# Up projections of a SwiGLU FFN token-major as seven products, with the weight sums made in DRAM by a chain of accumulating transfers

## The chip, the cores and the metric

The kernel runs on one core of a Trainium2 chip. The core has a matrix engine (TensorE, PE; its weight loads are shown apart as PEld), VectorE (DVE), ScalarE (ACT), GpSimd (POOL) and SyncE (SP), each with its own queue of instructions that it works through in order. Data moves between DRAM and the on-chip buffer (SBUF) by DMA transfers, which SP, ACT and POOL issue; TensorE writes its results into PSUM, of which the kernel uses eight tiles of 128 x 512 f32. The metric is the time of one execution in device microseconds.

## What is computed

Two layers of a decoder trunk on 512 tokens of width 1024. Each layer mixes tokens in four branches (the "mixer": a gated convolution, sparse attention, a gated recurrence, attention into a memory), adds the result to the residual `x`, and then runs a SwiGLU FFN of width 2816. The change is in the FFN:

```python
DEPTH = 2; SEQ = 512; D_MODEL = 1024; FFN_DIM = 2816
...
for l in range(DEPTH):
    x = hybrid_layer(x, ...)          # ends with:
...
    x = x + merged @ w_out
    hf = rmsnorm(x, norm_ffn)
    gate, up = jnp.split(hf @ ffn_w_up, 2, axis=-1)
    return x + (jax.nn.silu(gate) * up) @ ffn_w_down
```

All of it is f32.

## The kernel before

**Matrix products.** Every f32 operand is split in two: `hi`, a rounded copy that ScalarE makes, and `lo = x - f(hi)`, which VectorE makes. A product is three matmuls, hi x hi, hi x lo and lo x hi (`mm3`). Weights come from DRAM by loads on SP's queue into `w_raw` (two buffers, a third called `w_raw7` inside the FFN), are split into `w_hi` and `w_lo` (three buffers of 1024 columns each), and go to TensorE. `Chunk` does this for ordinary weights, `split` for the blocks of `down`.

**Order.** The code gives a program order and priorities; a scheduler fixes the order of each engine's queue when the kernel is built. Nothing is reordered at run time, so an instruction that waits holds all that stand behind it on its engine or queue.

**The FFN's up part.** `h` (the normalised input without its factor 1/rms, feature-major: 128 features on the partitions, 512 tokens along the row) is multiplied by chunks of 256 columns of the gate weights and of the up weights (`features`): 11 chunks `fc` of each, 2 x 8 x 3 matmuls of 512 columns per weight chunk. VectorE multiplies each result by `r_b`, the factor 1/rms broadcast over the partitions, ScalarE applies silu to the gates, VectorE multiplies by the up half, and the product, feature-major, is the left operand of the down projection.

**The FFN's down part.** `down` computes a 2 x 2 block product (token halves A11, A12, A21, A22; column halves C1, C2 of the weights) with seven products instead of eight (the Winograd form of Strassen's scheme). It needs sums of blocks on both sides: `operands` makes the left sums, and `weight_sums` the four right ones for each pair of 128-row blocks. Before the change, `weight_sums` loads the four blocks of one pair by a transfer on GpSimd's queue, VectorE makes four subtractions of 128 x 512, and a second GpSimd transfer stores the four sums in DRAM (`wt_dram`), from where `down` loads them. Layer 0 works in parts of 5 and 4 pairs with seven products and 2 pairs plainly (`add_down`, which also makes the next layer's input); layer 1 in parts of 6 and 5 pairs. Each `down` adds its PSUM banks into `acc` (tokens x 1024 columns) by `evict`, on VectorE. `acc` is zeroed by GpSimd in layer 0; in layer 1 it starts from `x`, brought in by `x_in` and turned by transposes on TensorE.

**What else the steps touch.** `conv_branch` (the mixer's gated convolution) multiplies the output of its first weight chunk by `r_b` into two `gate` tiles, near the start of each layer's mixer. GpSimd's queue carries, beside the weight sums, the loads of `x` in the FFN (`x_chunk`, `x_in`), a few zeroings of buffers in the mixer, the memset of `acc`, and two stores of the output. `norm_feature` makes `r_b` by matmuls against ones, `norm_token` the same factor with tokens on the partitions.

## Time and profile before

| | us |
|---|---|
| runs shown: median (lowest to highest of 3) | 2029.88 (2029.35 to 2030.08) |
| the profiled execution, its own time | 2032.38 |
| its span in the trace | 2030.6 |
| data moved by DMA | 269.86 MB, mean 133 GB/s |
| layer 0: mixer until 696.6, FFN from there | 696.6 |
| layer 1: FFN from about | 1676.6 |

The page gives, for each engine, the time in which it was busy and its share of the span. The chain of waits is followed back from the last instruction: at each step to what released it. The groups give, for one line, engine and shape: how often, the busy time in us, the mean duration of one in ns, and how long the engine had been idle before and for whom. Issues of transfers give the number, the size of each and the median time from issue to landing. Records of matmuls are pipelined and overlap; their spacing is read from the starts.

### The profile page before, as it was taken

How to read it: one execution, taken by the hardware profiler on the slowest of the kernel's cores; microseconds unless marked ns; L12 is line 12 of the kernel's file. 1: busy time of each engine (PE TensorE's matmuls, PEld its weight loads, DVE VectorE, ACT ScalarE, POOL GpSimd, SP SyncE). 2: the span in 40 equal slices, each digit the busy share in tenths (PEclk: the TensorE clock that was granted, in tenths of full speed). 3: DMA queues.
4: the chain of work that ended last, by engine and by line, in shares of the span. 5: the costliest groups of instructions: out<-in, count | busy, mean ns of one | idle time of the engine just before them, and what ended most of it. 6: DMA issues, size and time to landing. Idle time of an engine off the chain costs nothing.

```text
span 2030.6 us, 26664 instructions
## 1 busy us (share of the span) xinstructions
PE 2013.9 (99%) x10100; PEld 1690.6 (83%) x10100; DVE 1427.9 (70%) x2774; ACT 1067.2 (53%) x1914; POOL 45.1 (2%) x86
## 2 busy tenths in 40 slices
PE   8999999999999999999999999999999999999999
PEld 8998987778888888888889898877888788888887
DVE  5768898648776576666556889955678566666666
ACT  7653664866666433334345455477667544333333
POOL 0000000000000000000000000000000000000000
PEclk9999999999999999999999999999999999999999
DMA  7633231222233554664352223232222445566644
GB/s 253 210 92 104 68 104 62 83 63 83 83 113 124 196 210 150 229 218 143 105 182 72 91 79 94 73 94 68 79 80 80 151 140 192 187 212 220 222 148 155
DMA packets 192159, 269.86 MB, mean 133 GB/s; under 512 B 5774, under 2 KB 157920, under 8 KB 189088
## 3 DMA queue, kind: packets, MB, share of 16 engines
q1 hardware_dynamic: 176320, 208.51, 32.2%
q0 software_dynamic: 9568, 46.80, 6.2%
q10 hardware_dynamic: 6144, 12.87, 1.7%
q8 instruction: 79, 1.29, 0.3%
q14 instruction: 48, 0.39, 0.1%
HBM read 232.50 MB, written 35.65 MB: 132 GB/s over the span
## 4 chain that ended last, share of the span: by engine, by line
PE 95%; DVE 2%; ACT 1%; DMA 1%; issue 0%; DVEq 0%; SPq 0%; ACTq 0%
PE mm L277 28%; PE mm L279 28%; PE mm L278 27%; PE at L279 1%; PE at L278 1%; PE at L277 1%; PE tr L737 1%; PE tr L731 1%; PE at L705 1%; PE at L706 1%; ACT w_hi L97 1%; PE tr L279 1%; PE tr L277 1%; PE tr L278 1%; DVE acc L1264 0%; DVE w_lo L230 0%
## 5 line engine op out<-in xcount | busy, mean ns | idle before, releaser
L277 PE MATMUL mm<-h_hi,w_hi 128*128 128x512 f32 x1664 | 651.7, 393 | 3.1 <-ACT w_hi L97 2.4
L278 PE MATMUL mm<-h_lo,w_hi 128*128 128x512 f32 x1664 | 652.6, 392 | 0.0
L279 PE MATMUL mm<-h_hi,w_lo 128*128 128x512 f32 x1664 | 648.5, 392 | 1.7 <-DVE w_lo L230 1.6
L97 ACT ACTIVATE w_hi<-w_raw 128x1024 fp32r<-128x1024 f32 (+1 forms) x384 | 394.7, 1033 | 383.8 <-PE mm L278 242.7
L230 DVE TENSOR_TENSOR w_lo<-w_raw,w_hi 128x1024 fp32r<-128x1024 f32 x304 | 369.6, 1219 | 198.5 <-ACT w_hi L97 198.0
L277 PEld LDWEIGHTS mm<-h_hi,w_hi 128*128 128x128 f32 x1664 | 313.0, 188 | 69.4 <-ACT w_hi L97 3.9
L279 PEld LDWEIGHTS mm<-h_hi,w_lo 128*128 128x128 f32 x1664 | 313.1, 188 | 66.8 <-DVE w_lo L230 3.2
L278 PEld LDWEIGHTS mm<-h_lo,w_hi 128*128 128x128 f32 x1664 | 313.0, 188 | 63.2 <-issue 0.2
L1088 DVE TENSOR_TENSOR w_lo<-w_raw,w_hi 128x1024 fp32r<-128x1024 f32 (+1 forms) x80 | 86.5, 1090 | 64.1 <-ACT w_hi L97 64.1
L279 PE MATMUL mm<-w_hi,h_lo 128*128 128x256 f32 (+2 forms) x368 | 109.3, 297 | 0.0
L278 PE MATMUL mm<-w_lo,h_hi 128*128 128x256 f32 (+2 forms) x368 | 109.1, 297 | 0.0
L277 PE MATMUL mm<-w_hi,h_hi 128*128 128x256 f32 (+2 forms) x368 | 108.7, 298 | 0.0
L97 ACT ACTIVATE a_hi<-fg 128x512 fp32r<-128x512 f32 (+1 forms) x84 | 48.5, 580 | 112.7 <-DVE fg L1238 84.8
L277 PE MATMUL mm<-y_hi,w_hi 128*128 128x512 f32 x256 | 100.5, 394 | 1.2 <-ACT y_hi L97 1.2
L279 PE MATMUL mm<-y_hi,w_lo 128*128 128x512 f32 x256 | 100.4, 393 | 0.0
L278 PE MATMUL mm<-y_lo,w_hi 128*128 128x512 f32 x256 | 100.3, 392 | 0.0
L97 ACT ACTIVATE prob<-prob,small 128x128 f32<-128x128 f32 (+3 forms) x128 | 68.9, 554 | 17.5 <-DVE small L720 12.6
L278 PEld LDWEIGHTS mm<-w_lo,h_hi 128*128 128x128 f32 x368 | 70.1, 191 | 2.1
L279 PEld LDWEIGHTS mm<-w_hi,h_lo 128*128 128x128 f32 x368 | 70.1, 191 | 1.9
L277 PEld LDWEIGHTS mm<-w_hi,h_hi 128*128 128x128 f32 x368 | 69.8, 191 | 1.9
L97 ACT ACTIVATE gate_e<-gate 128x512 f32<-128x512 f32 x64 | 40.2, 628 | 43.5 <-DVE gate L537 42.8
L278 PE MATMUL mm<-w_lo,a_hi 128*128 128x512 f32 x160 | 62.2, 389 | 0.0
(404 smaller groups left out, 3298.6 us busy)
## 6 DMA issues: line engine op xcount, KB each, us to landing
w_raw<-in_w_in_dram SPq DMA_DIRECT2D x72, 1024.0 KB, 5.2
w_raw<-in_ffn_w_up_dram SPq DMA_DIRECT2D x44, 1024.0 KB, 5.2
w_raw<-in_ffn_w_down_dram POOLq DMA_DIRECT2D x20, 1024.0 KB, 5.9
w_sums<-w_raw POOLq DMA_DIRECT2D x20, 1024.0 KB, 4.5
w_raw<-in_w_lift_dram SPq DMA_DIRECT2D x32, 512.0 KB, 3.4
w_raw<-w_sums SPq DMA_DIRECT2D x20, 768.0 KB, 4.2
w_raw<-in_ffn_w_down_dram SPq DMA_DIRECT2D x9, 1024.0 KB, 6.0
w_raw<-in_mem_w_kv_dram SPq DMA_DIRECT2D x8, 1024.0 KB, 5.2
```

What stands on the lines that cost most here:

```text
L97: i = act.activation(dst, src, func, **kw)
L230: dve.tensor_sub(lo, raw[:, k:e], f(hi))
L277: return [pe.matmul(ps, ah, bh, start=first, stop=False, skip_group_check=more), pe.matmul(ps, ah, bl, start=False, stop=False, skip_group ...
L278: pe.matmul(ps, ah, bl, start=False, stop=False, skip_group_check=more),
L279: pe.matmul(ps, al, bh, start=False, stop=last, skip_group_check=more)]
L705: return [pe.matmul(ps, q[:, hh, s], k[0][:, :n], start=True, stop=False), pe.matmul(ps, q[:, hh, s], k[1][:, :n], start=False, stop=True)]
L706: pe.matmul(ps, q[:, hh, s], k[1][:, :n], start=False, stop=True)]
L731: pe.transpose(pp[:, (2 * e + i) * P:(2 * e + i + 1) * P], probs[2 * i + e][:, b * P:(b + 1) * P], ident)
L737: pe.matmul(pv[e * HD:(e + 1) * HD, :], vt[:, b, :], pt[:, b, e * 2 * P:(e + 1) * 2 * P], start=b == 0, stop=b == t)
L1088: follow(dve.tensor_sub(lo[:, k:k + n, :], src, f(hi[:, k:k + n, :])), earlier)
```

## The change

- `up_set` replaces the chunks of the up part. One set covers 512 gate columns and the 512 up columns that belong to them. Its left blocks are halves of the tokens and of the 1024 features, its right blocks the upper and lower half of the features for gate and for up. It makes seven products (A11, A12, S2, S1, S3, S4, A22) of 24 matmuls each, with the tokens on the partitions of the result ("token-major"). There are five sets; the last 256 features go through `up_plain`, 256 columns wide.
- `left_sums` makes the left sums S1 to S4 of `h` once per layer on VectorE and ScalarE.
- The results being token-major, the factor 1/rms becomes a scalar per partition (`r_t`, `nr_t`); `norm_feature` is no longer called here, `norm_token` is. `turned` brings the products back to feature-major by transposes on TensorE and a copy on ScalarE.
- `weight_sums` is called once per layer, from the convolution branch, for all sums of the layer: the up sums into a new DRAM tensor `up_sums` and the down sums into `w_sums`. Each sum is a plain copy DRAM to DRAM and an accumulating transfer on top of it, both on GpSimd's queue, and each transfer waits for the landing of the one before. The signs are arranged so that only additions are needed; `operands`, `left_sums` and `evict` carry the other signs.
- `down` works on pairs (0, 1, 10), (2, 3, 4, 5) and (6, 7, 8, 9), in layer 0 with 8 and 9 plain.
- The zeroings that stood on GpSimd in the mixer move to VectorE; the loads of `x` in the FFN move from GpSimd's queue to SP's. The memset of `acc` stays on GpSimd.

```diff
                 for u, ps in zip(us, features(w, h, (0, 1))):
-                    pool.memset(u[:, 0:2], 0.0)
+                    dve.memset(u[:, 0:2], 0.0)
                     with tc.high_priority(offset=AHEAD):
-                        dve.tensor_mul(u[:, 2:], ps, r_b)
+                        i = dve.tensor_mul(u[:, 2:], ps, r_b)
+                if c2 == 0:
+                    weight_sums(l, i)
...
-    def weight_sums(fp, l, i):
-        raw = fp.tile([P, 4, 512], F32, name="w_raw7")
-        nc.gpsimd.dma_start(raw.rearrange("p (e c) n -> p e (c n)", e=2),
-                            ffn_w_down[l][2 * i * P:2 * (i + 1) * P, :].rearrange("(e p) n -> p e n", p=P))
-        b12, b11, b22, b21 = (raw[:, j, :] for j in range(4))
-        dve.tensor_sub(b11, b12, b11)
-        dve.tensor_sub(b12, b22, b12)
-        dve.tensor_sub(b22, b22, b11)
-        dve.tensor_sub(b21, b21, b22)
-        nc.gpsimd.dma_start(wt_dram[l, :, i], raw)
+    def weight_sums(l, gate):
+        last = [gate]
+        def move(dst, src, **kw):
+            i = nc.gpsimd.dma_start(dst, src, **kw)
+            tc.add_manual_dep(i.ins, last[0].ins.name, sync, reason="one by one")
+            last[0] = i
+        def four(sums, b11, b21, b12, b22):
+            t3, t1, t2, t4 = sums
+            for dst, one, two in ((t1, b11, b12), (t2, t1, b22), (t4, t2, b21), (t3, b12, b22)):
+                for add in (False, True):
+                    for d, x, y in zip(dst, one, two):
+                        if add:
+                            move(d, y, accum_op=OP.add)
+                        else:
+                            move(d, x)
+        for n in range(FF // 512):
+            def block(e, g):
+                c = g * FF + n * 512
+                b = ffn_w_up[l][e * 512:(e + 1) * 512, c:c + 512].rearrange("(k p) n -> p k n", p=P)
+                return [b[:, 0:2, :], b[:, 2:4, :]]
+            four([[wu_dram[l, n, j][:, 0:2, :], wu_dram[l, n, j][:, 2:4, :]] for j in range(4)],
+                 *(block(e, g) for g in range(2) for e in range(2)))
+        rows = ffn_w_down[l].rearrange("(i e p) n -> p i e n", e=2, p=P)
+        for i in ((0, 2), (10, 11), (2, 4), (4, 6), (6, 8)) + (((8, 10),) if l == DEPTH - 1 else ()):
+            i = slice(*i)
+            four([[wt_dram[l, :, i, j]] for j in range(4)],
+                 *([rows[:, i, e, c]] for c in (C1, C2) for e in range(2)))
...
+    def left_sums(fp, h):
+        raw = fp.tile([P, NT, D], F32, name="acc").rearrange("p a b -> p (a b)").rearrange("p (k s) -> p k s", s=S)
+        for k in range(0, KD, 2):
+            dve.tensor_add(raw[:, k:k + 2, :], f(h[0][:, k:k + 2, :]), f(h[1][:, k:k + 2, :]))
+        g0, g1 = raw[:, 0:4, :], raw[:, 4:8, :]
+        s2, s1 = g0[:, :, :HALF], g0[:, :, HALF:]
+        dve.tensor_sub(s1, g1[:, :, HALF:], s1)
+        dve.scalar_tensor_tensor(s2, s1, -1.0, s2, op0=OP.mult, op1=OP.subtract)
...
+            def product(bank, o, src, first):
+                raw = raw_tile(fp).rearrange("p (k n) -> p k n", n=512)
+                nc.sync.dma_start(raw, src)
+                for e in range(2):
+                    w = split([(0, 2, raw[:, 2 * e:2 * e + 2, :])])
+                    for t, ps in enumerate(bank):
+                        for j in range(2):
+                            k = 2 * e + j
+                            a = [where[o](x, k)[:, t * P:(t + 1) * P] for x in lefts]
+                            mm3(ps, a, w[j], first and k == 0, k == 3, not first)
...
+                product(ba, A11, block(0, 0), True)
+                g = copies(ba, "fg", 2)
+                product(bb, A12, block(1, 0), True)
...
+                        dve.tensor_add(g[t], g[t], bb[t])
+                        A(g[t], g[t], AF.Silu, scale=r_t[:, t:t + 1])
...
+                product(ba, S2, sums[SUM2], False)
+                v = copies(ba, "fu", 4)
+                product(bc, S1, sums[SUM1], True)
+                u = copies(bc, "fu", 4)
+                product(ba, S3, sums[SUM3], False)
...
+                product(bc, S4, block(1, 1), False)
...
+                        dve.tensor_add(v[t], v[t], bc[t])
+                        dve.scalar_tensor_tensor(v[t], v[t], nr_t[:, t:t + 1], g[t], op0=OP.mult, op1=OP.mult)
+                product(ba, A22, sums[SUM4], False)
...
+            def turned(us, j, name="fx", bufs=2):
+                ps = tr_ps()
+                for t in range(NT):
+                    pe.transpose(ps[:, t * P:(t + 1) * P], us[t][:, j * P:(j + 1) * P], ident)
+                g = fp.tile([P, S], F32, name=name, bufs=bufs)
+                A(g, ps, AF.Copy)
+                return g
...
+            for part, idx in enumerate(((0, 1, 10), (2, 3, 4, 5), (6, 7, 8, 9))):
+                if part == 0:
+                    us = up_set(0, lambda: kept.append(turned(up_plain(0, [at_ps(), at_ps()]), 0, "fy", 1)))
...
+                    acc = fp.tile([P, NT, D], F32, name="acc")
+                    if last:
+                        x_in(0)
+                        x_in(4)
+                    else:
+                        pool.memset(acc, 0.0)
+                    ops.append(operands(fp, kept[0], turned(pls, 0), False, N_OPS))
+                else:
+                    ops = pairs_of(up_set(2 * part - 1), False)
+                    ops += pairs_of(up_set(2 * part), part == 2 and not last)
```

More of the change, by code (lines that the diff above doesn't have):

```diff
@@ L1128, in operands, with down @@
         return hi, lo
-    def down(fp, w2d, sums, ops, evict):
+    def down(fp, w2d, sums, idx, ops, evict):
         n = len(ops)
@@ L1184, in down @@
             raw = raw_of(2 * m)
-            nc.sync.dma_start(raw[:, 0::2, :], sums[:, i0:i0 + m, SUM3])
-            nc.sync.dma_start(raw[:, 1::2, :], rows[:, i0:i0 + m, 1, C2])
+            nc.sync.dma_start(raw[:, 0::2, :], sums[:, idx[i0]:idx[i0] + m, SUM3])
+            nc.sync.dma_start(raw[:, 1::2, :], rows[:, idx[i0]:idx[i0] + m, 1, C2])
             for i in range(m):
@@ new lines, in ffn @@
+            hs, h1 = left_sums(fp, h)
+            where = {A11: lambda x, k: x[0][:, k, :HALF], A12: lambda x, k: x[0][:, 4 + k, :HALF],
+                     A22: lambda x, k: x[0][:, 4 + k, HALF:], S2: lambda x, k: x[1][:, k, :],
+                     S1: lambda x, k: x[2][:, k, :], S4: lambda x, k: x[1][:, 4 + k, :],
+                     S3: lambda x, k: x[1][:, 8 + k, :]}
+            lefts = [(h[e], hs[e], h1[e]) for e in range(2)]
+            def product(bank, o, src, first):
+                raw = raw_tile(fp).rearrange("p (k n) -> p k n", n=512)
+                nc.sync.dma_start(raw, src)
+                for e in range(2):
+                    w = split([(0, 2, raw[:, 2 * e:2 * e + 2, :])])
[4 more added lines that the diff above has]
+                            mm3(ps, a, w[j], first and k == 0, k == 3, not first)
@@ new lines, in turned, with pairs_of @@
+            def turned(us, j, name="fx", bufs=2):
+                ps = tr_ps()
+                for t in range(NT):
+                    pe.transpose(ps[:, t * P:(t + 1) * P], us[t][:, j * P:(j + 1) * P], ident)
+                g = fp.tile([P, S], F32, name=name, bufs=bufs)
+                A(g, ps, AF.Copy)
+                return g
+            def pairs_of(us, plain):
+                return [operands(fp, *(turned(us, 2 * i + j) for j in range(2)), plain, N_OPS) for i in range(2)]
+            acc = None
@@ L1268, in evict @@
                     return adds
-                down(fp, wd, wt_dram[l, :, f0:f1], ops, evict)
-        return None, None
+                n = 2 if part == 2 and not last else len(idx)
+                down(fp, ffn_w_down[l], wt_dram[l], idx[:n], ops[:n], evict)
+            if last:
+                return None, None
+            h2, ssq2 = new_h(), new_ssq()
+            add_down(x_chunk, ffn_w_down[l][idx[n] * 256:(idx[-1] + 1) * 256, :], [Pairs(t) for t in zip(*ops[n:])],
+                     2 * len(ops[n:]), acc, h2, ssq2, lambda c: g_mix(l + 1, c))
+            return h2, ssq2
     for l in range(DEPTH):
```

149 lines of the change are left out of this document (96 added, 53 removed).

## The prediction

> **What bounds the kernel now.** I read the page's busy times and its chain of waits first, then the busy time of each engine by stretches, then single rows.
>
> ```profile
> PE 2013.9 (99%) x10100; PEld 1690.6 (83%) x10100; DVE 1427.9 (70%) x2774; ACT 1067.2 (53%) x1914; POOL 45.1 (2%) x86
> ...
> PE 95%; DVE 2%; ACT 1%; DMA 1%; issue 0%; DVEq 0%; SPq 0%; ACTq 0%
> ```
>
> TensorE is the bound: busy for 99% of the span and 95% of the chain that ended last. The stretches say that this holds in the FFN too: layer 0's up projections (697 to 806), the part of `down` behind them (806 to 860), and the tail with layer 1's end. Columns: length, busy time and instructions of PE, weight loads, VectorE, ScalarE and GpSimd, the granted clock, the DMA engines' share and rate.
>
> ```profile
> 697.00:806.00 109.00, 108.82 (x480) 89.74 (x480) 73.30 (x103) 40.81 (x54) 5.61 (x9) 1.00 0.56 195
> 806.00:860.00 54.00, 53.65 (x237) 43.97 (x236) 39.26 (x50) 21.50 (x24) 1.97 (x3) 1.00 0.60 200
> ...
> 1820.00:2030.00 210.00, 206.12 (x908) 169.88 (x906) 136.00 (x180) 73.84 (x89) 7.41 (x12) 1.00 0.55 188
> ```
>
> TensorE waits 0.5 us in the first two together. A seven-product stage (the second row) already runs at 99% of PE with VectorE at 39.26 / 54 = 73%. So a matmul that goes is worth its spacing, if nothing new makes TensorE wait. Matmul records last 0.39 us but overlap; the spacing is read from starts.
>
> ```profile
> 1729.74 0.39 PE L279 MATMUL mm<-h_hi,w_lo 128*128 128x512 f32 x1
> ...
> 1741.98 0.39 PE L279 MATMUL mm<-h_hi,w_lo 128*128 128x512 f32 x1
> ...
> 63.34 0.28 PE L278 MATMUL mm<-w_lo,mt_hi 128*128 128x256 f32 x1
> ...
> 66.33 0.28 PE L279 MATMUL mm<-w_hi,mt_lo 128*128 128x256 f32 x1
> ...
> 1721.49 1.31 PE tr L1220 x12
> ...
> L1220 PE MATMUL tr<-ident,w_raw 128*128 128x128 f32 x32 | 4.1, 272 | 0.0
> ```
>
> Between the first two starts lie 54 steps: 12.24 / 54 = 0.2267 us for 512 columns. Between the next two lie 25 steps: 2.99 / 25 = 0.120 us for 256 columns. Twelve transposes take 1.31 us of the chain: 0.109 us each, though one's own record lasts 272 ns.
>
> **The change, part by part.** *Matmuls.* Before, one layer's up projections are 11 chunks x 2 weights x 2 x 8 x 3 = 1056 matmuls of 512 columns. After, they are 5 sets x 7 products x 24 = 840, and 192 of 256 columns for the last 256 features. Over two layers: 432 fewer of 512 (-97.9 us) and 384 more of 256 (+46.1). The results are now token-major, so each set is turned by 16 transposes and the rest by 8: 88 a layer, 176 x 0.109 = +19.2. If a transpose cost the 0.272 us of its own record it would be +47.9; the twelve above stand among matmuls as the new ones will, so I take 0.109. The `norm_feature` matmuls that go and the `norm_token` ones that come are a dozen: nothing. `down` multiplies as many pairs by seven products as before (9 and 11). Sum: **-32.6 us**.
>
> *VectorE and ScalarE.*
>
> ```profile
> L230 DVE TENSOR_TENSOR w_lo<-w_raw,w_hi 128x1024 fp32r<-128x1024 f32 x187 | 228.1, 1222 | 139.4 <-ACT w_hi L97 139.2
> ...
> L1235 DVE TENSOR_TENSOR fg<-mm,rstd 128x512 f32<-128x512 f32 x44 | 29.8, 688 | 24.7 <-PE mm L279 24.5
> ...
> L1102 DVE TENSOR_TENSOR w_raw<-w_raw 128x512 f32<-128x512 f32 x20 | 13.7, 686 | 0.2
> L97 ACT ACTIVATE w_hi<-w_raw 128x1024 fp32r<-128x1024 f32 x247 | 260.6, 1058 | 292.6 <-PE mm L278 186.7 <-PE mm L279 32.6 <-PE at L279 27.4
> ```
>
> Seven blocks instead of four for the same weights: 148 splits of 1024 for 88. A set has 14 splits (14 x 1.222 = 17.1 us of VectorE), 10 operations of 512 (6.9) and two `operands` (about 4 each, from the same 0.69): 32 us beside 168 x 0.2267 + 1.7 = 39.8 of TensorE, 80%. ScalarE has 14 x 1.058 and about 20 operations of 0.63: 27 us. The 80 subtractions of the weight sums (55 us) go. So these edits cost nothing under TensorE's time, but with less cover than the 73% above. `left_sums`, 12 VectorE operations of 1024 (14.7 us) and four ScalarE copies, lies under A11, A12 and the first plain product, (48 x 0.2267 + 96 x 0.120) = 22.4 us; the first product that needs it comes behind them. Where the cover fails is at seams: end of a set, plain part to `down`, and one `down` more in each layer (three where layer 1 had two). Lower bound 0; upper bound twice the idle share of the worst stretch above (3.9 of 210), over two FFNs of some 354 us (1676.6 to 2030.6 in layer 1): 26. I take **+8** (about 2 us at each of four seams, near the rows' 0.35 in 54).
>
> *The chain of sums.* GpSimd now issues 120 transfers in layer 0 and 128 in layer 1, each waiting for the one before: 16 for each of five up blocks, 8 for each down group, half plain copies, half additions into DRAM, 512 KB but for eight of 256. The first waits for the convolution's second product:
>
> ```profile
> 109.69 0.67 DVE L594 TENSOR_TENSOR gate<-mm,rstd 128x512 f32<-128x512 f32 x1
> ...
> 1121.01 0.69 DVE L594 TENSOR_TENSOR gate<-mm,rstd 128x512 f32<-128x512 f32 x1
> ...
> L277 PE MATMUL mm<-mg_hi,w_hi x64: 389/389/389, 653.1 to 695.9; 128*128 128x512 f32 x64
> L277 PE MATMUL mm<-h_hi,w_hi x160: 389/389/497, 696.6 to 805.7; 128*128 128x512 f32 x160
> ...
> L277 PE MATMUL mm<-mg_hi,w_hi x64: 389/389/389, 1633.3 to 1676.1; 128*128 128x512 f32 x64
> ```
>
> So the chain starts at 110.4 and 1121.7, and the FFNs at 696.6 and about 1676.6. In the built kernel's order layer 0's memset of `acc` stands on GpSimd *behind all 120 links*; the first eviction of `down` adds into `acc`, and behind those adds VectorE holds every weight split, so TensorE stops soon after. That eviction is due at 696.6 + 38.1 (a set) + 23.0 (two plain products) + 2.6 (24 transposes) + 8.2 (36 matmuls) = 768.5. Allowed: (768.5 - 110.4) / 120 = **5.48 us a link**. In layer 1 there is no memset; SP's load of the first down sums waits for link 96, due about 1676.6 + 38.1 + 23.0 + 2.6, so (1740.3 - 1121.7) / 96 = 6.44. The first up sums (link 16) are never near. What a link costs is not in the trace; the nearest rows:
>
> ```profile
> w_raw<-in_ffn_w_down_dram POOLq DMA_DIRECT2D x20, 1024.0 KB, 5.9
> w_sums<-w_raw POOLq DMA_DIRECT2D x20, 1024.0 KB, 4.5
> ...
> w_raw<-in_ffn_w_down_dram SPq DMA_DIRECT2D x9, 1024.0 KB, 6.0
> ...
> w_raw<-in_ffn_w_down_dram SPq DMA_DIRECT2D x15, 512.0 KB, 3.3
> ...
> 725.97 0.56 POOL L1103 DMA_DIRECT2D w_sums<-w_raw  x1 [13.06 <-DVE w_raw L1102]
> 731.01 0.71 POOL L1096 DMA_DIRECT2D w_raw<-in_ffn_w_down_dram  x1 [4.49 <-DMA w_sums<-w_raw]
> ...
> POOL w_raw L1096 <- DMA w_sums<-w_raw: 60.8, 14, 5.3
> ```
>
> The last rows are a link already: GpSimd issues a 1 MB store and the next transfer waits for it, 0.56 + 60.8 / 14 = 4.9 us with the DMA engines at 56 to 65%. A 512 KB copy lies between the load's 3.3 and that 4.9: I take 4.2. An addition reads two blocks and writes one: at least the copy's 4.2, at most a 1 MB load and a 1 MB store link one after the other, 10.8; I take the 1 MB load, 5.9, since the block written is small beside what is read. Mean 5.05 (3.8 to 7.9): layer 0's chain ends at 110.4 + 606 = 716, 52 us early. Cost **0**; without that cover, 120 x (link - 5.48).
>
> The Trainium skill's "DMA: Bandwidth & Descriptors", "Anatomy of one DMA — SWDGE (gpsimd) path", gives about 2.0 us and the bytes at 436 GB/s for a transfer of this queue. Its "Collectives: The Full Stack", "The bandwidth ceiling: the fold count and why AG ≠ RS ≠ AR", says an adding transfer reads two sources and so moves at half the rate. By both (an estimate) a link is 3.2 or 4.4, mean 3.8, and the sum is the same; the 4.9 measured for 1 MB is a little over the first rule's 4.4.
>
> *What the chain does to the loads.* Through the mixers it adds traffic where the DMA engines are about a quarter busy (0.28 in the first row).
>
> ```profile
> 110.00:250.00 140.00, 140.00 (x882) 126.45 (x881) 113.16 (x306) 71.44 (x170) 0.20 (x2) 1.00 0.28 87
> ...
> w_raw<-in_w_in_dram SPq DMA_DIRECT2D x72, 1024.0 KB, 5.2
> ...
> w_raw<-in_w_lift_dram SPq DMA_DIRECT2D x32, 512.0 KB, 3.4
> ...
> w_raw<-in_w_out_dram SPq DMA_DIRECT2D x8, 1024.0 KB, 5.0
> ...
> SPq L219 <- DVE w_lo L230: 1277.7, 132, 19.9
> ...
> ACT w_hi L97 <- DMA w_raw<-in_w_in_dram: 8.7, 5, 3.5
> ```
>
> Loads are issued when a buffer comes free, about 9.7 us after the one before, and a split waited for one only five times. I take **+4** (0 to 15: each of the 112 loads of those three rows late by 0.14). The sums' loads are 7 MB a set, 1 MB per 5.4 us, three buffers deep. The FFN's x chunks move from GpSimd's queue to SP's, since GpSimd's is now held by waits; the zeroings move to VectorE: some 24 short operations, nothing.
>
> The profiled execution took 2032.4 us, 2.5 over the median. 2032.4 - 32.6 + 8 + 0 + 4 = 2011.8; against the median, **2009**.
>
> **The rivals.** *A, the chain is late (slower).* Everything above 5.48 us a link is paid 120 times, in front of the memset. For it: the additions are unmeasured, and links run beside the mixers' loads; against it: the 4.9 us for twice the bytes. With additions at 8.2 (a 1 MB load, and half a store of 4.5) and copies at 4.2, a link is 6.2: 120 x 0.72 = 86, 2095. It turns gain into loss from (2029.9 - 2009) / 120 = 0.17 over, at 5.65.
>
> A rule that would lengthen links is in the skill's "SBUF — State Buffer", "Who interferes with whom": VectorE's two-port copies block GpSimd, which writes the descriptors. Here GpSimd's issues last 0.56 and 0.71 us in the rows above with VectorE 70% busy, which speaks against it; one blocked copy of 1.2 a link would give 6.25 and 2009 + 92 = 2101, a case inside A with 0.02 of its chance.
>
> *B, contention.* The chain slows the mixers' loads until splits wait. 0.4 us at 112 loads is 45, in place of 4: 2050. For it: lift chunks of 5.4 us of TensorE follow 3.4 us loads; against it: the five waits above.
>
> *C, seams.* VectorE at 80% is late by 0.2 us at each of 140 half products: 28 us in place of 8, 2029, no change. Against it: the 73% stage lost 0.35 us in 54.
>
> *D, transposes at 0.272*: 2009 + 29 = 2038. The twelve above speak against it.
>
> **How the numbers follow.** Forecast 0.59, A 0.25, B 0.07, C 0.07, D 0.02. 2009 is the likeliest; its own range is 1997 (seams 0, loads 0: 2032.4 - 32.6 - 2.5) to 2024 (seams 18, loads 9). The whole range goes up to 2068, a link of 5.97 in A, leaving most of the rest of A out. What a measurement can tell from no change is about 0.2%, 4 us. Faster: the forecast and small parts of B and C, 0.64; same: most of C, the turn of A, 0.06; slower: 0.30.
>
> **What would show it.** Right: TensorE about 33 us less busy, GpSimd's transfers 4 to 6 us apart, the memset of `acc` ahead of about 760, no wait of VectorE's `acc` adds on GpSimd, up sets of about 40 us. Wrong: transfers over 5.5 us apart with TensorE idle in front of layer 0's first eviction (A); idle at splits behind loads in the mixers (B); idle spread over the sets (C); transposes in rows of 0.27 (D).

## The result, and the profile after

| | before | after |
|---|---|---|
| median of 4 runs, us | 2029.62 (2029.22 to 2030.08) | 2115.89 (2107.61 to 2121.16) |
| profiled execution: time, span, us | 2032.4, 2030.6 | 2107.6, 2105.5 |

The change made the kernel slower: 1.0421 times the time (95% interval 1.0384 to 1.0459), 86 us more where 21 fewer were forecast. One of the four executions of the run with the memset alone, further down, was slow (2485.56 us at a clock of 0.75), so its figures are the median of the other three, 2048.92, where the later expectations name 2049.8, and its stretches are read from other runs. The page of after shows the same two parts as before: busy times, and the engines' shares of the chain that ended last.

```profile
PE 1999.7 (95%) x10240; PEld 1680.3 (80%) x10240; DVE 1476.5 (70%) x2814; ACT 1190.6 (57%) x2100; POOL 230.2 (11%) x264
...
PE 59%; DMA 33%; issue 3%; DVE 3%; ACT 2%; POOL 0%; SPq 0%; DVEq 0%; POOLq 0%; ACTq 0%
```

TensorE's instructions went up by 140, as the count of the prediction has it (432 fewer of 512 columns, 384 more of 256, 176 transposes and a dozen of the norms). But TensorE is busy for 95% of the span, and a third of the chain is DMA. The waits say where (engine, line, what for; total, times, longest):

```profile
POOL up_sums L1107 <- DMA up_sums<-in_ffn_w_up_dram: 641.4, 115, 8.2
...
PE mm L283 <- DVE acc L1407: 63.7, 2, 62.9
DVE acc L1407 <- POOL acc L1392: 63.6, 1, 63.6
```

One wait of 63.6 us: VectorE's first addition into `acc` waits for GpSimd's memset, and TensorE's matmul for VectorE. GpSimd's own timeline, and after it the stretches around the stall (length, busy PE, weight loads, VectorE, ScalarE, GpSimd, granted clock, DMA share and rate):

```profile
831.53 0.72 POOL L1107 DMA_DIRECT2D w_sums<-in_ffn_w_down_dram  x1 [5.42 <-DMA w_sums<-in_ffn_w_down_dram]
836.19 1.13 POOL L1107 DMA_DIRECT2D w_sums<-in_ffn_w_down_dram  x1 [3.94 <-DMA w_sums<-in_ffn_w_down_dram]
836.89 3.95 POOL L1392 MEMSET acc<- 128x4096 f32 x1
```

```profile
697.00:770.00 73.00, 70.53 (x409) 62.45 (x408) 50.95 (x61) 41.15 (x57) 10.80 (x12) 0.98 0.82 231
770.00:840.00 70.00, 8.42 (x38) 6.29 (x36) 7.19 (x14) 7.71 (x15) 14.89 (x14) 0.60 0.53 108
840.00:900.00 60.00, 56.16 (x237) 45.57 (x238) 40.84 (x50) 26.49 (x31) 0.84 (x1) 0.96 0.57 189
```

The chain starts at 113.4 and issues its last link at 836.2: 723 us for 119 spacings, 6.07 each. The memset stands behind them, so `acc` is ready at 840.9 where VectorE wanted it at 777.3. That is rival A. What one link takes is read from the starts: a copy is issued in 0.72 us, an addition in 1.14 to 1.16.

```profile
518.17 0.72 POOL L1107 DMA_DIRECT2D up_sums<-in_ffn_w_up_dram  x1 [6.51 <-issue]
522.43 1.16 POOL L1107 DMA_DIRECT2D up_sums<-in_ffn_w_up_dram  x1 [3.54 <-DMA up_sums<-in_ffn_w_up_dram]
529.22 1.14 POOL L1107 DMA_DIRECT2D up_sums<-in_ffn_w_up_dram  x1 [5.62 <-DMA up_sums<-in_ffn_w_up_dram]
535.76 0.57 POOL L1107 DMA_DIRECT2D up_sums<-up_sums  x1 [5.41 <-DMA up_sums<-in_ffn_w_up_dram]
```

A copy of 4.26, then additions of 6.79 and 6.54: this is a quick piece of the chain. Over the whole of layer 0's chain a copy takes 5.0 us on average and an addition 7.2, from start to start (eight of the 120 links are of 256 KB). There is a second loss, in layer 1, where no memset waits: the stretch 1800 to 1840, SP's queue in it, and two pieces of the chain.

```profile
1800.00:1840.00 40.00, 26.88 (x134) 22.66 (x134) 20.68 (x35) 21.40 (x37) 6.70 (x7) 0.87 0.72 189
```

```profile
SPq L1272 <- PE tr L1276: 9.9, 1, 9.9
```

```profile
1815.99 5.60 DMA w_raw<-x_spill
...
1825.26 5.35 DMA w_raw<-in_ffn_w_down_dram
```

TensorE idles 13 of these 40 us. `x_in`'s two loads of 1 MB now stand on SP's queue, in a buffer that the weights use too; the second waits until the first has been transposed, and `down`'s first weights wait behind it.

### The profile page after: what moved, and what is told of

Same layout as the page of the kernel before. It is cut to its first block, busy times and chain, and to the rows that moved or that the text cites. A ratio compares the mean times of both kernels' runs of the same rounds, so it can differ in the third digit from the quotient of the medians.

```text
span 2105.5 us, 27445 instructions
## 1 busy us (share of the span) xinstructions
PE 1999.7 (95%) x10240; PEld 1680.3 (80%) x10240; DVE 1476.5 (70%) x2814; ACT 1190.6 (57%) x2100; POOL 230.2 (11%) x264
## 4 chain that ended last, share of the span: by engine, by line
PE 59%; DMA 33%; issue 3%; DVE 3%; ACT 2%; POOL 0%; SPq 0%; DVEq 0%; POOLq 0%; ACTq 0%
DMA up_sums<-in_ffn_w_up_dram 18%; PE mm L283 15%; PE mm L284 15%; PE mm L285 15%; DMA w_sums<-in_ffn_w_down_dram 8%; DMA up_sums<-up_sums 4%; PE at L285 2%; PE at L284 2%; PE at L283 2%; DMA w_sums<-w_sums 2%; DVE acc L1407 1%; ACT w_hi L99 1%; PE tr L283 1%; DVE w_lo L1097 1%; PE tr L284 1%
## 5 line engine op out<-in xcount | busy, mean ns | idle before, releaser
L99 ACT ACTIVATE w_hi<-w_raw 128x1024 fp32r<-128x1024 f32 (+2 forms) x444 | 456.5, 1035 | 368.9 <-PE mm L284 117.1
L283 PE MATMUL mm<-h_hi,w_hi 128*128 128x512 f32 x960 | 378.1, 395 | 2.8 <-ACT w_hi L99 1.7
L284 PE MATMUL mm<-h_lo,w_hi 128*128 128x512 f32 x960 | 378.4, 394 | 0.0
L285 PE MATMUL mm<-h_hi,w_lo 128*128 128x512 f32 x960 | 376.4, 393 | 1.3 <-DVE w_lo L236 1.3
L1097 DVE TENSOR_TENSOR w_lo<-w_raw,w_hi 128x1024 fp32r<-128x1024 f32 (+1 forms) x220 | 256.1, 1175 | 155.8 <-ACT w_hi L99 155.8
L236 DVE TENSOR_TENSOR w_lo<-w_raw,w_hi 128x1024 fp32r<-128x1024 f32 (+1 forms) x224 | 272.0, 1217 | 113.1 <-ACT w_hi L99 111.9
L1107 POOL DMA_DIRECT2D up_sums<-in_ffn_w_up_dram x120 | 121.4, 1012 | 1086.0 <-DMA up_sums<-in_ffn_w_up_dram 516.4
L283 PEld LDWEIGHTS mm<-h_hi,w_hi 128*128 128x128 f32 x960 | 180.8, 188 | 40.4 <-ACT w_hi L99 2.2
L285 PEld LDWEIGHTS mm<-h_hi,w_lo 128*128 128x128 f32 x960 | 180.9, 189 | 37.9 <-DVE w_lo L236 1.7
L284 PEld LDWEIGHTS mm<-h_lo,w_hi 128*128 128x128 f32 x960 | 180.8, 188 | 35.6 <-issue 0.2
L284 PE MATMUL mm<-w_lo,h_hi 128*128 128x256 f32 (+2 forms) x600 | 197.4, 329 | 2.1 <-DVE w_lo L1097 2.1
L283 PEld LDWEIGHTS mm<-w_hi,h_hi 128*128 128x128 f32 x600 | 113.7, 191 | 10.2 <-ACT w_hi L99 0.9
```

What stands on the lines that cost most here:

```text
L99: i = act.activation(dst, src, func, **kw)
L236: dve.tensor_sub(lo, raw[:, k:e], f(hi))
L283: return [pe.matmul(ps, ah, bh, start=first, stop=False, skip_group_check=more), pe.matmul(ps, ah, bl, start=False, stop=False, skip_group ...
L284: pe.matmul(ps, ah, bl, start=False, stop=False, skip_group_check=more),
L285: pe.matmul(ps, al, bh, start=False, stop=last, skip_group_check=more)]
L1097: follow(dve.tensor_sub(lo[:, k:k + n, :], src, f(hi[:, k:k + n, :])), earlier)
```

## The experiments

Times are medians, each set against the runs of the kernel before on the same chip (2028.8 to 2029.8); "over before" is that difference. After is 86.3 over before.

### The memset alone

```diff
-                        pool.memset(acc, 0.0)
+                        dve.memset(acc, 0.0)
```

> One edit: layer 0's memset of acc goes from GpSimd to VectorE, so nothing of down's first eviction is queued behind the 120 links any more; the links themselves stay as they are. Theory (the late memset alone makes the stall; the links are slow but otherwise in time): the wait of 63.6 us of VectorE's acc addition on GpSimd is gone, no other wait takes its place (SP's first down sums need only link 96, which came at about 700), the granted clock stays at 1.00 there, and the time falls from 2107.6 by 63.6 and some 5 to 10 us of slow clock: about 2037 (2030 to 2048). The links' spacing stays near 6.05 us. Rival (links of 6 us are too late for other users as well): SP's loads of w_sums wait instead, and the time stays above 2080. Rival (what is slow is the FFN's new order itself): the wait moves to other places of the FFN and the time stays above 2060.

Measured: 2048.92, 20.2 over before (ratio 1.0096, 1.008 to 1.0113). One word moved takes 66 us out, so the late memset is the stall. But 2048.9 lies above the 2030 to 2048 expected: 20 us over before remain where the prediction, with its chain in time, had 21 under it.

### Larger links, the memset left where it was

```diff
-                return [b[:, 0:2, :], b[:, 2:4, :]]
-            four([[wu_dram[l, n, j][:, 0:2, :], wu_dram[l, n, j][:, 2:4, :]] for j in range(4)],
+                return [b]
+            four([[wu_dram[l, n, j]] for j in range(4)],
```

> The memset of acc stays on GpSimd behind the whole chain; only the size of the up links changes: 1 MB instead of twice 512 KB, so layer 0's chain has 80 links for 120 with the same bytes. From the links measured by themselves (1 MB: copy 5.6, addition 9.3 alone, 6.8 and 9.9 beside loads; 512 KB: 5.3 and 7.9 beside loads; 256 KB some 4.7) the chain takes 20 x 6.2 + 20 x 9.6 + 32 x 6.3 + 8 x 4.7 = 555 us, from 113 to about 668, some 100 us ahead of the first eviction of down. Theory (the stall is the chain's length past the memset's due time, nothing else): the acc addition waits for nothing on GpSimd and the time is that of the run with the memset on VectorE, about 2047 (2038 to 2056). Rival (bytes set the chain's length, not links): the chain ends near 830 as before and the time stays at 2110. Rival (1 MB links hold the loads up more): no stall at acc, but over 2060.

Measured: 2046.81, 17.2 over before (1.0081, 1.0064 to 1.0099). GpSimd's timeline has the last link at 674.7 (668 was worked out), and now the memset waits for VectorE's `left_sums`, not VectorE for the memset:

```profile
674.66 1.15 POOL L1107 DMA_DIRECT2D w_sums<-in_ffn_w_down_dram  x1 [6.12 <-DMA w_sums<-in_ffn_w_down_dram]
727.20 3.53 POOL L1392 MEMSET acc<- 128x4096 f32 x1 [51.40 <-DVE hs_lo L1247]
```

The same bytes in 80 links instead of 120 end 160 us earlier, and the stall goes. The chain's length past one due time sets the loss; with a third fewer links and the bytes unchanged, that length falls from 723 to 558 us.

### Links by themselves

The kernel holds nothing but two runs of links, the second beside paced loads.

```diff
...
+    for r in range(6):
+        for k in (slice(0, 2), slice(2, 4)):
+            move(sums[0][:, k, :], block(0, r * 512)[:, k, :])
+        for k in (slice(0, 2), slice(2, 4)):
+            move(sums[0][:, k, :], block(1, r * 512)[:, k, :], accum_op=OP.add)
+    for r in range(6):
+        move(sums[1], block(0, r * 512))
+        move(sums[1], block(1, r * 512), accum_op=OP.add)
...
```

> None of the reference is computed but a copy of x: the kernel only issues links from GpSimd's queue, each behind the one before, twice: first alone, then beside loads of 1 MB of w_in on SP's queue, one every 9 to 10 us as in the mixers. In each half: 12 copies and 12 additions of 512 KB from rows of 2 KB, 6 of each with 1 MB, 6 of each with 256 KB. Theory (an addition into DRAM is slow by itself): alone, a copy of 512 KB takes 4 to 4.5 us from start to start and an addition 6 to 7, and beside the loads each is at most 0.5 us longer. Rival (the links are slow because the mixers' loads take the DMA engines): alone 4 and 5, as the sum of the prediction had it or less, beside the loads 5 and 7. The three sizes give the fixed part: if 256 KB takes more than two thirds of what 512 KB takes, a link is mostly fixed time, and 1 MB links would cost less per byte.

GpSimd's timeline in the first half, with no other transfer running: additions, copies and the next addition of 512 KB; then a 1 MB copy, an addition, and the next copy.

```profile
68.20 1.14 POOL L85 DMA_DIRECT2D sums<-in_ffn_w_up_dram  x1 [5.67 <-DMA sums<-in_ffn_w_up_dram]
74.94 0.72 POOL L85 DMA_DIRECT2D sums<-in_ffn_w_up_dram  x1 [5.60 <-DMA sums<-in_ffn_w_up_dram]
79.17 0.71 POOL L85 DMA_DIRECT2D sums<-in_ffn_w_up_dram  x1 [3.52 <-DMA sums<-in_ffn_w_up_dram]
83.63 1.16 POOL L85 DMA_DIRECT2D sums<-in_ffn_w_up_dram  x1 [3.74 <-DMA sums<-in_ffn_w_up_dram]
...
187.03 0.75 POOL L85 DMA_DIRECT2D sums<-in_ffn_w_up_dram  x1 [8.41 <-DMA sums<-in_ffn_w_up_dram]
192.62 1.14 POOL L85 DMA_DIRECT2D sums<-in_ffn_w_up_dram  x1 [4.84 <-DMA sums<-in_ffn_w_up_dram]
201.98 0.77 POOL L85 DMA_DIRECT2D sums<-in_ffn_w_up_dram  x1 [8.23 <-DMA sums<-in_ffn_w_up_dram]
```

Means of start to start, in us (the 512 KB copies alone hold two of 8.1 and 7.2 at the very start; their median is 4.27):

| | copy 256 KB, 512 KB, 1 MB | addition 256 KB, 512 KB, 1 MB |
|---|---|---|
| alone | 3.3, 4.8, 5.6 | 4.6, 6.9, 9.3 |
| beside loads | 4.9, 5.3, 6.8 | 4.6, 7.9, 9.9 |

An addition of 512 KB takes 6.9 us with nothing beside it, so it is slow by itself. Beside the loads it takes 0.9 more, and a copy 1.0 more than its median alone, so the theory's 0.5 was short and its rival has a part too. From 512 KB to 1 MB an addition grows by 2.4 us, and from 256 KB to 512 KB, half the step in bytes, by 2.3: one fixed part doesn't fit all three sizes. An addition of 256 KB takes two thirds of one of 512 KB, so the runs don't show that an addition is mostly fixed time; but the larger link is the cheaper one per byte at every step. VectorE does nothing in this kernel and GpSimd's issues last 0.72 and 1.14 us as in after: VectorE's work isn't what lengthens them.

### No chain at all

```diff
-                if c2 == 0:
-                    weight_sums(l, i)
...
-                product(ba, S2, sums[SUM2], False)
+                product(ba, S2, block(0, 1), False)
```

> The transfers that make the sums of weights are left out altogether (all 248), and the products that used sums read plain blocks of the same weights in the same sizes, so the output differs from the reference's; the matmuls, splits, transposes and loads stay. Theory (only the late memset and x's loads cost something, the chain's traffic costs the mixers nothing): the acc addition waits for nothing, mixers take 582 to 587 us and 623 us as in both kernels, and the time is that of the run with the memset on VectorE within 6 us: about 2035 (2025 to 2045). Rival (the chain's traffic slows the loads by contention): over 15 us below that run. Rival (the seven-product order itself is what costs): above 2060.

The loads keep their bytes, though one of `down`'s is made in two pieces. Measured: 2037.21, 8.4 over before (1.0037, 1.0024 to 1.005) and 11.7 under the memset alone. The time is inside 2025 to 2045, but the theory had put this run within 6 us of the other. So the chain's traffic costs something, and the seven-product FFN is slow with no sums to wait for. The traces (table under "The sum") put 4.7 of the 11.7 into the FFNs and nothing into layer 1's mixer; layer 0's mixer takes 700.6 us without a chain and 699.3 to 705.5 with it. TensorE in the stretches at the start of the first `down` of either layer:

```profile
755.00:780.00 25.00, 20.70 (x127) 18.20 (x126) 14.52 (x28) 14.56 (x26) 0.00 (x0) 0.93 0.20 69
...
1738.00:1770.00 32.00, 22.24 (x110) 18.33 (x109) 17.64 (x32) 20.21 (x36) 0.00 (x0) 0.84 0.30 98
```

4.3 us idle in layer 0, 9.8 in layer 1, at a lowered clock besides. Pieces of the chain at the two places (start, length, what):

```profile
766.44 1.22 DVE w_lo L1095
...
768.00 0.94 DVE a_lo L1145 x2
...
769.27 0.52 DVE fu L1359 x2
...
770.99 0.27 DVE fu L1359
771.31 0.50 PE mm L283
...
1752.81 4.85 DMA w_raw<-x_spill
...
1760.50 3.64 DMA w_raw<-in_ffn_w_down_dram
```

In layer 0, `down`'s first matmul waits for a bank that the second plain part's gate (`fu`) still reads; that gate stands on VectorE behind the operands of the set. In layer 1 the `x` loads come on top. The next runs take these one at a time.

### The second plain part inside the set

```diff
-                    us = up_set(0, lambda: kept.append(turned(up_plain(0, [at_ps(), at_ps()]), 0, "fy", 1)))
-                    b0 = mm_ps()
-                    pls = up_plain(1, [b0, tr_ps()])
...
+                    def plain1():
+                        pls = up_plain(1, [mm_ps(), tr_ps()])
+                        pair.append(operands(fp, kept[0], turned(pls, 0), False, N_OPS))
+
+                    us = up_set(0, plain0, plain1)
...
```

> Memset on VectorE; and the second plain part of the first set (96 matmuls of 256 columns, its gate and its operands) stands behind the set's third product instead of at the set's end, so that VectorE's and ScalarE's work for it lies under four more products. Theory (TensorE's 6 us of lost time between 755 and 780 in layer 0, and as much in layer 1, are the plain part's gate and operands waiting behind a backlog of VectorE with no product left to hide them): the stretch loses under 3 us in each layer and the time is 5 to 9 us under the run with the memset alone (2049.8), about 2043. Rival (the loss is the start of down itself, its first split and the turned operands of the set): within 3 us of 2049.8.

Measured: 2036.50, 6.9 over before (1.0038, 1.0024 to 1.0053), 13 under the memset alone, more than expected. The stretch in layer 0, which holds chain links here:

```profile
755.00:780.00 25.00, 22.94 (x106) 18.10 (x105) 22.99 (x35) 16.03 (x25) 3.60 (x4) 1.00 0.75 186
```

VectorE is busy 23.0 us of 25 where it was 14.5 without a chain, and the clock stays at 1.00; 2.1 us of idle are left. In the traces the FFNs take 349.3 and 353.7 us, where the same code with the plain part at the end takes 352.5 and 361.1: 10.6 of the 13 us. The rest is within what one trace differs from another in layer 0's mixer.

### The loads of x later

```diff
-                xs = fp.tile([P, 2048], F32, name="w_raw7")
-                nc.sync.dma_start(xs.rearrange("p (m t) -> p m t", t=S), x_dram[:, m0:m0 + 4, :])
+                xs = [x_chunk(m0 + m) for m in range(4)]
...
+                    if last:
+                        x_in(4 * part - 4)
                     ops = pairs_of(up_set(2 * part - 1), False)
```

> Memset on VectorE in both layers; layer 1's x no longer takes a buffer of the weights ahead of down, but comes in eight loads of 256 KB into fu's four buffers, four behind the first down and four behind the second, and VectorE adds it to acc. Theory (the two 1 MB loads of x take one of the three weight buffers and SP's turn just when down's first weights are due: 15 us of lost time at 1740 to 1770 in the run without a chain, of which the seam itself is 6): 7 to 11 us under the run with the memset alone (2049.8), about 2041. Rival (the same megabytes and transposes cost as much wherever they stand): within 3 us of 2049.8.

Measured: 2037.35, 7.8 over before (1.0038, 1.0025 to 1.0051), 12 under the memset alone, a little more than expected. Layer 1's FFN takes 349.1 us where it took 361.1 in after, 12.0 less. Idle in 1738 to 1770 is 3.5 us, where it was 9.8 without a chain:

```profile
1738.00:1770.00 32.00, 28.50 (x164) 24.39 (x162) 19.20 (x34) 17.21 (x30) 4.47 (x6) 0.89 0.76 212
```

Asking for the same two 1 MB loads earlier instead, inside the up set, was a miss:

```diff
+                        if last:
+                            acc_box.append(fp.tile([P, NT, D], F32, name="acc"))
+                            x_in(0)
...
+                    if last:
+                        x_in(4)
```

> As the run with the memset on VectorE, and layer 1's two loads of x (1 MB each, into one buffer) are asked for earlier: the first beside the second product, the second behind the first up set, instead of both just ahead of down's first weights. Theory (SP's queue stands still behind the second of them until the first is transposed, and down's first loads come late behind it): the idle 13 us of TensorE between 1800 and 1840 go to under 3, its clock stays at 1.00 there, and the time is 12 to 17 us under the run with the memset alone: about 2022. Rival (the gap at the start of down is the first loads of down anyway, whatever stands ahead of them): less than 4 us of difference.

Measured: 2045.78, only 3 under the memset alone. The gap at the start of `down` did shrink (3.9 us idle between 1738 and 1770, at a clock of 1.00), but it moved: the load took a weight buffer in the set, and a split waited 6.1 us for its `up_sums`, with TensorE idle 8.1 us between 1700 and 1720. An up set loads 1 MB for each 5.4 us of TensorE and had no room for it.

### The zeroings, and the chain's traffic, in the kernel before

Both runs change the kernel before.

```diff
-                    pool.memset(u[:, 0:2], 0.0)
+                    dve.memset(u[:, 0:2], 0.0)
...
-                pool.memset(f(ikS[1][HD:P, :]), 0.0)
+                dve.memset(f(ikS[1][HD:P, :]), 0.0)
```

> The kernel before with one edit of the change alone: the mixers' zeroings (gate, k_lo, ik_lo, chunk_mult, a_intra) go from GpSimd to VectorE; everything else stays, the FFN too. Theory (the zeroings of gate and ik_lo wait at 83 to 86 for the transfer kv<-kv, whose buffer they take over; on VectorE that wait holds qg_lo and TensorE behind it, and a slower granted clock follows): TensorE loses 4 to 6 us more between 80 and 100 than the 2.4 of before, and the time is 3 to 7 us over the kernel before: about 2034. Rival (a dozen short operations are nothing, as the prediction had it): within 1.5 us of 2029.6.

Measured: 2035.83, 6.1 over before (1.0027, 1.0017 to 1.0038). In before it was GpSimd that waited for the transfer `kv<-kv`, at no cost:

```profile
POOL ik_lo L748 <- DMA kv<-kv: 24.1, 1, 24.1
```

With the zeroings on VectorE, its timeline and the stretches show what stands behind them:

```profile
85.47 0.48 DVE L748 MEMSET ik_lo<- 64x512 f32 x1 [2.61 <-DMA kv<-kv]
85.99 0.74 DVE L635 SCALAR_TENSOR_TENSOR qg_lo<-mm,prm,qg_hi 128x512 fp32r<-128x512 f32 x1
```

```profile
84.00:88.00 4.00, 1.21 (x5) 1.21 (x6) 1.96 (x6) 1.19 (x5) 0.00 (x0) 0.65 0.05 19
88.00:92.00 4.00, 4.00 (x21) 4.00 (x20) 1.02 (x5) 0.63 (x4) 0.00 (x0) 0.50 0.02 4
92.00:96.00 4.00, 4.00 (x23) 4.00 (x22) 1.76 (x11) 3.19 (x13) 0.00 (x0) 0.57 0.01 2
```

TensorE idles 2.8 us, and then its clock is at 0.50 to 0.57 for eight: 21 and 23 matmuls in 4 us where the same stretches of before hold 35 and 29. In the traces, layer 0's mixer takes 700.0 us for 696.4, and every other part as long as before: 3.6 of the 6.1 us between the medians are seen there.

With the first 80 links of each layer beside it, their sums read by nobody:

```diff
+                if c2 == 0:
+                    links(l, i)
```

> As the run with the zeroings on VectorE, and beside it the first 80 links of each layer's chain (the sums of the up blocks, 512 KB each, into DRAM that nothing reads) run through the mixers; the FFN is that of the kernel before. Against the run with the zeroings alone this is the price of the chain's traffic. Theory (the loads in the mixers stay hidden under TensorE): 0 to 4 us more, 2034 to 2038. Rival (contention, as the 12.6 us between the run without a chain and the run with the memset on VectorE suggest): 7 to 12 us more, 2041 to 2046, with idle of TensorE behind late loads in the mixers.

Measured: 2040.49, 10.7 over before (1.0049, 1.0036 to 1.0061), 4.6 over the zeroings alone, between the two theories. The stretches of the mixer without links, and with them:

```profile
110.00:400.00 290.00, 286.99 (x1575) 245.62 (x1574) 232.04 (x588) 162.41 (x354) 0.00 (x0) 1.00 0.27 84
```

```profile
110.00:400.00 290.00, 284.87 (x1561) 243.27 (x1560) 230.45 (x584) 160.87 (x353) 41.79 (x47) 1.00 0.69 167
```

The DMA share goes from 0.27 to 0.69, and TensorE loses 2.1 us in 290. So the mixers mostly hide the chain. The 11.7 us between the runs with and without a chain hold the FFNs too, where up sets have the loads with the least slack.

### All of it together

The larger links, layer 0's memset on GpSimd and layer 1's on VectorE, the plain part inside, `x` later, and `ik_lo` back on GpSimd:

> All of it together: 1 MB up links, layer 0's memset on GpSimd behind the shorter chain and layer 1's on VectorE, the second plain part inside the set, x later in small loads, and the zeroing of the indexer's ik_lo back on GpSimd (on VectorE it waited 3 us for the transfer kv<-kv at 83 to 86, and qg_lo and with it TensorE behind it). If the parts add up: 2049.8 - 8 (x) - 7 (plain part) - 3 (ik_lo) - 3 (fewer links) = about 2029, the time of the kernel before (2020 to 2037). Rival (the seams only move on to the next wait): above 2038.

Measured: 2031.83 (2024.62 to 2036.48), 2.3 over before (1.0006, 0.9996 to 1.0016): no difference. The wait for `kv<-kv` was still there, now on `gate`'s zeroing (2.5 us on VectorE). So:

```diff
-                    dve.memset(u[:, 0:2], 0.0)
+                    (dve if c2 else pool).memset(u[:, 0:2], 0.0)
```

> As the run with all four repairs, and the first zeroing of gate (in front of the chain on its queue) goes back to GpSimd too, since there gate on VectorE took over the wait for kv<-kv that ik_lo had (2.5 us, with TensorE idle 2.3 and a clock of 0.78). Theory: the lost time between 80 and 100 falls from 4.4 us to the 2.4 of the kernel before, and the median from 2031.8 by 2 to 4 us to about 2029. Rival (the spread of that run, 2024.6 to 2036.5, comes from elsewhere, and so does its median): 2031 to 2033.

Measured: 2026.24, 3.5 under before (0.9986, 0.9978 to 0.9995), and 5.6 under the run ahead of it. Last, the order of the pairs in the first `down`, which now takes them as one and two instead of two and one:

```diff
-            for part, idx in enumerate(((0, 1, 10), (2, 3, 4, 5), (6, 7, 8, 9))):
+            for part, idx in enumerate(((10, 0, 1), (2, 3, 4, 5), (6, 7, 8, 9))):
...
-                    ops += pair
+                    ops = pair + ops
```

> As the run before it (four repairs, gate's first zeroing on GpSimd), and down's first part takes the pair of the plain columns (10) first, since its operands are ready a product earlier than those of the set (pairs 0 and 1); so TensorE has 12 matmuls while the set's 16 transposes, fx and a_lo are made. Theory (what is left at 755 to 770 and 1735 to 1750, 4.0 and 5.5 us of lost time, is that latency): 3 to 7 us under 2026.2, about 2021. Rival (the seam is the first split of down's own weights, or the bank that the last gate still reads): within 1.5 us of 2026.2.

Measured: 2024.33 (2019.57 to 2026.56), 5.3 under before (0.9968, 0.9959 to 0.9977): a little under both kernels. The step itself gave 1.9, between theory and rival; in the traces the two FFNs shorten by 1.5 and 1.4. The prologue and the starts of `down` in it:

```profile
80.00:100.00 20.00, 20.00 (x152) 19.10 (x151) 14.84 (x61) 15.50 (x52) 0.66 (x3) 1.00 0.36 126
755.00:780.00 25.00, 23.83 (x110) 18.68 (x109) 22.72 (x35) 15.55 (x23) 0.00 (x0) 1.00 0.37 116
1735.00:1760.00 25.00, 24.31 (x115) 18.79 (x114) 22.10 (x34) 14.98 (x23) 0.00 (x0) 1.00 0.53 160
```

No idle and a full clock at 80 to 100; 1.2 and 0.7 us left at the two seams.

## Why the prediction was wrong, point by point

**The chain, the step that failed.** The sum took 4.2 us for a copy, 5.9 for an addition, 5.05 for the mean, and a cost of 0. In layer 0 a copy took 5.0, an addition 7.2, the mean was 6.07. About half of the 1.02 between the means is the addition itself: alone it takes 6.9, which adds 0.5, while the copy's 4.27 is as estimated. The reason given, that an addition is like a 1 MB load "since the block written is small beside what is read", fell: 6.9 lies between that load and the 10.8 of the upper bound. The other half comes on top in the kernel, beside its loads. The sum had a term for what the chain does to the mixers' loads, and none for what the loads do to the chain, which only rival A names. With links as they are alone, 5.6 on average, the chain would have run only some 14 us past the limit (an estimate: 0.12 x 120).

Past the limit of 5.48, (6.07 - 5.48) x 120 = 71 us; the wait is 63.6, since the eviction was wanted 8.8 us later than worked out (777.3 for 768.5) and the chain started 3.0 later; the memset's own 4.0 and the last link, which has only to be issued and not to land, nearly cancel. Moving the memset took out 66. So rival A's place, threshold and form of price held; its size of link (6.2) was a little high. That its 2095 lies near the 2115.9 is in part luck: its stall of 86 was too long by 22, and its other terms promised a gain of 21 where 20 were lost. The choice of the lower row for a cost that nothing showed, 120 times in a row with 8% to spare, was the error, and the range's top of 2068 cut rival A off at a link of 5.97.

The estimate from the Trainium skill ("DMA: Bandwidth & Descriptors" with "Collectives: The Full Stack", the sections named there) was 3.2 and 4.4. Alone on the chip the two took 4.27 and 6.9, so the runs don't bear its size out; that an addition takes well over a copy holds, 1.6 times as long where the estimate has 1.4. The case from the Trainium skill's "SBUF — State Buffer" didn't occur: GpSimd's issues are as long with VectorE silent.

**Matmuls, -32.6.** The counts are confirmed. The gain can't be read by itself, but in the last run each FFN is 7 us shorter than before with its seams still in it (348.1 for 355.3 us in layer 0, 343.1 for 349.8 in layer 1, by the table below). Matmuls and seams together had been put at -12 for each.

**Seams, +8 (0 to 26).** Too small. The plain part's end alone cost 13 us by its run, of which the traces show 10.6. The prediction took the idle share of a stage in full flow as a measure for the place where one form of work ends and the next begins; there VectorE's 80% turned into a backlog with no product to hide it.

**Moves costed at nothing.** The `x` loads on SP cost 12 us, and the zeroings on VectorE 6.1. In both the prediction counted the operations and not the waits that they carry: GpSimd's 24.1 us wait for `kv<-kv` stood in the trace of before, and `x_in`'s single buffer in the code.

**Contention, +4 (0 to 15).** The right size: 4.6 for 80 links a layer, 11.7 at most for all. A 1 MB load of the mixers takes 1.8 us longer in after than the 5.2 it took before, and most of it is hidden (loads, size of each, median us to landing):

```profile
w_raw<-in_w_in_dram SPq DMA_DIRECT2D x72, 1024.0 KB, 7.0
```

**The sum.** 20.2 over before without the stall, less 12.4, 13.2, 6.1 and 11.7 for these four, is -23.2. The matmuls alone were put at -32.6, so some 9 us of other seams would be left. The parts don't quite add up in the other direction: with three of them mended and the chain left in, -11.5 would follow, and -3.5 was measured. The traces, one execution each, say where the time lies. A layer's mixer ends here with the start of the last matmul that reads `mg`, its FFN with the start of the last that reads `a_hi` or `a_lo`.

| us | mixer 0 | FFN 0 | mixer 1 | FFN 1 |
|---|---|---|---|---|
| before | 696.4 | 355.3 | 624.9 | 349.8 |
| before, zeroings on VectorE | 700.0 | 355.4 | 624.9 | 349.8 |
| the same with 80 links a layer | 700.9 | 356.6 | 626.4 | 349.8 |
| after | 700.4 | 415.4 | 624.6 | 361.1 |
| memset on VectorE, `x` asked for earlier | 705.0 | 352.5 | 624.6 | 360.4 |
| 1 MB links, memset on GpSimd | 702.8 | 351.0 | 631.4 | 356.2 |
| no chain | 700.6 | 352.1 | 624.6 | 356.8 |
| second plain part inside | 699.3 | 349.3 | 624.6 | 353.7 |
| `x` later | 705.5 | 352.6 | 625.3 | 349.1 |
| all together | 697.3 | 349.5 | 625.1 | 346.5 |
| `gate`'s first zeroing on GpSimd | 696.7 | 349.6 | 627.1 | 344.5 |
| pair 10 first | 697.3 | 348.1 | 631.0 | 343.1 |

The last run gains 14 us in its two FFNs and gives 6.1 back in layer 1's mixer. With 1 MB links that mixer takes 625.1 to 631.4, with 512 KB links 624.6 to 626.4; a stall shown below is part of it, and the rest is open.

## What to carry to other kernels

Before work goes onto a queue as a chain of waits, list everything that the program puts behind it and the time at which each is wanted; a memset that depends on nothing in the chain still waits for all of it. When an operation is moved to another engine, its wait moves with it and is then paid by whatever that engine does next, so look up what it waited for in the old place, not how long it ran. Measure an operation that repeats a hundred times before pricing it, alone and beside the traffic that it will run with; and try fewer, larger transfers first, since 80 links in place of 120 took the stall away with the bytes unchanged.

## What the runs showed of the hardware

The granted clock of TensorE falls in an idle time of only 2.8 us, and how long it stays low differs from run to run. In the run with the zeroings on VectorE the three rows from 84 to 96 have 0.65, 0.50 and 0.57: if the clock is either 1 or a half, that is 10.2 us at half. In the run with links beside them TensorE idles as long in the same place, and the mean clock of the stretch is 0.91 for 0.74, some 3.6 us at half (both estimates from these rows):

```profile
80.00:100.00 20.00, 17.17 (x113) 16.96 (x112) 10.23 (x48) 10.09 (x33) 0.00 (x0) 0.74 0.22 84
80.00:100.00 20.00, 17.12 (x130) 16.78 (x129) 11.62 (x52) 12.27 (x40) 0.00 (x0) 0.91 0.25 91
```

The Trainium skill's "TensorE: Matmul & The Clock Gate", section "What's actually happening", has the half rate follow an idle window of about 3.4 us and end after a busy one as long. The traces agree with the half rate; the idle time here was shorter, and the slow time about one such window in one run and three in the other.

With nothing beside it, an addition into DRAM of 256 KB, 512 KB and 1 MB takes 4.6, 6.9 and 9.3 us where a copy takes 3.3, 4.3 (the median) and 5.6, each from start to start. From rows of 2 KB an addition of 512 KB is issued in 1.14 us, a copy in 0.72.

A load that runs beside a 1 MB addition can come late. In the run with larger links one load of 1 MB, 5.2 us at the median before and 6.6 in this run, took 11.24 (a piece of its chain):

```profile
1228.71 11.24 DMA w_raw<-in_w_in_dram
```

GpSimd had issued a 1 MB addition at 1227.85 and waited for it until 1238.54, and TensorE stood idle for 4.4 us behind the load. That the addition held the load up is argued from this overlap alone; the run with all together had an addition in the same place and no idle time of TensorE there (25.00 of 25 us busy between 1225 and 1250).
